# Turning key and value rows on VectorE and through DRAM instead of on TensorE, in a two-layer decoder step

## The chip, the cores and the metric

The kernel runs on one core of one Trainium2 chip. The metric is the device time of one execution in microseconds; a run's figure is the median of several executions. TensorE is the matrix engine (PE in the profile, its weight loads PEld), VectorE is DVE, ScalarE is ACT, GpSimd is POOL, and SyncE is SP, whose queue issues most of the DMAs.

## The reference

A step of a two-layer trunk over 512 prompt tokens and 32 new tokens of eight sequences (544 token columns). Layer 0 mixes tokens by a convolution, layer 1 by an attention without softmax, and each is followed by a gated feed-forward part. The change lies in layer 1, where key and value rows are outputs of their own and values also enter the attention:

```python
qkv = (h @ attn_w_qkv[a]).reshape(b, t, 3, N_HEADS, HEAD_DIM)
q, k, v = qkv[:, :, 0], qkv[:, :, 1], qkv[:, :, 2]
...
z = jnp.einsum('bqhd,bkhd->bhqk', q, k) * (HEAD_DIM ** -0.5)
z = z + bias[None, :, None, None]
log_fail = jnp.where(valid, jax.nn.log_sigmoid(-z), 0.0)
after = lax.cumsum(log_fail, axis=3, reverse=True) - log_fail
weights = jnp.where(valid, jnp.exp(jax.nn.log_sigmoid(z) + after), 0.0)
out = jnp.einsum('bhqk,bkhd->bqhd', weights, v)
...
new_k.append(k)
new_v.append(v)
```

`k_rows_p` and `v_rows_p` are these rows for the prompt: 512 tokens by 1024 features in fp32, one token's features side by side.

## The kernel before

Activations lie with features on the 128 partitions (eight chunks of 128 features) and the 544 tokens along the free dimension. Every projection multiplies fp32 weights as a high and a low part, so a chunk of 128 outputs takes three matmuls for each of eight input chunks. It is done in two halves of tokens, 256 and 288 columns, into PSUM tiles `acc` of which two exist.

The kernel's stages follow each other. Layer 1's attention stage, which holds the whole change, begins with the first key projection (L2126 to L2128) and ends with the output projection's first quarter. In it `Plan` collects operations with an engine, a cost in us, and what they read and write; `run` then walks a clock of its own, takes for each engine the ready operation with the best mix of start and urgency, and emits its instructions at once. So each engine's program order comes out of these costs, and any edit of an operation re-orders all of them. The projections are `fill`: they are taken when nothing else is ready for TensorE. SP's DMAs are operations too (`"sp"`, cost 3.0, the queue free again after 0.7).

For chunk `c` and half `h`, `keys(c, h)` projects, copies the result to `kT` on ScalarE (L2164), and `values(c, h)` copies it to a tile `vT` (L2178). Both then call `to_rows` (L2150): two TensorE transposes of 128x128 (L2156) into the PSUM tile `one`, so that tokens are on partitions. For keys a VectorE copy (L2170) brings the rows to `kr` and one DMA per half (L2171) stores them with runs of 512 bytes. For values a VectorE copy (L2182) brings them to `vtok[c % 3]`, which the attention reads, and one DMA per chunk stores `vtok` (L2185).

`pair(c)` is the prompt's attention for the two heads of chunk `c`: logits (L2388), the weights on ScalarE, GpSimd and VectorE (running sums L2418), transposes of the weights into PSUM tiles `t` (L2430), and `products` (L2450), which multiply them with `vtok`. `page_logits` and `sequence` are the new tokens' attention over cached pages, gathered by GpSimd (L2018) into three buffers; the pages are transposed (L2246) into `t` as well. The PSUM tile `one` also serves the new tokens' small steps. Weights for the projections are loaded by `Ring.load` on SP (L361) into two buffers `raw`, and split into high and low parts (L398 on ScalarE, L401 on VectorE) five slots ahead of their use; the load of a buffer is issued right behind the L401 that reads it last.

Of the kernel before, what the change touches and what calls it, by code (L numbers as in the profile page):

```python
# [9 lines left out]
F32 = mybir.dt.float32  # L10
# [7 lines left out]
P = 128  # L18
D = 1024
NC = D // P  # L20
SEQ = 512
# [13 lines left out]
SA = (0, 256)  # L35
# [215 lines left out]
def tile_trunk(  # L251
# [217 lines left out]
    def uid(s):  # L469
        _n[0] += 1  # L470
        return f"{s}_{_n[0]}"
# [262 lines left out]
    def psum(tag):  # L734
        def make():
            if tag == "acc":
                taken.append(tag)
            return bank(tag, uid(tag))

        return plan.tile(tag, banks[tag], make)  # L740
# [1310 lines left out]
    act_table("natural_log_exp_and_others")  # L2051

    close(ps_cm)
    kpv = k_p[0, 0].rearrange("(b p) h d -> p b (h d)", p=P)
    vpv = v_p[0, 0].rearrange("(b p) h d -> p b (h d)", p=P)
    ksv = k_s.rearrange("o b i h d -> (o b i) (h d)")
    vsv = v_s.rearrange("o b i h d -> (o b i) (h d)")
# [14 lines left out]
    HALF = [slice(0, HD), slice(HD, P)]  # L2072
    ps_cm, ps = open_pool("ps_va", space=PSUM)
    banks.clear()
    banks.update(acc=2, one=1, dz=1, av=1, z=2, t=1)


    plan = Plan()
# [13 lines left out]
    def sbuf(tag, w, bufs, dt=F32, pool_=va):  # L2092
        return plan.tile(tag, bufs, lambda: pool_.tile([P, w], dt, tag=tag, name=uid(tag), bufs=bufs))
# [10 lines left out]
    def acost(n):  # L2104
        return 0.1 + n * 0.95e-3
# [41 lines left out]
            prepare(slot + SPLIT_BUFS)  # L2147
        return pt

    def to_rows(src, r):  # L2150

        rows = psum("one")

        def turn():
            for b in range(2):
                pe.transpose(rows()[:, b * P:(b + 1) * P], src(b), ident)  # L2156

        plan.op("pe", 0.22, turn, r=r, w=[rows])
        return rows, (lambda: rows()[:, :2 * P].rearrange("p (b d) -> p b d", b=2))

    def keys(c, h):
        c0, n = (SA, SB)[h]
        pt = project(k0 + TURNS.index(("k", c)), h)
        plan.op("act", acost(256), lambda: act.copy(kT[:, c, c0:c0 + 256], pt()[:, :256]),  # L2164
                r=[pt], w=[("k", c, h)] + ([("ktp", i) for i in range(4)] if c >= 4 else []))
        if h:
            plan.op("act", 0.2, lambda: act.copy(kT_s[:, c, :], pt()[:, 256:n]), r=[pt], w=[("kT_s", c)])
        rows, src = to_rows(lambda b: kT[:, c, c0 + b * P:c0 + (b + 1) * P], [("k", c, h)])
        kr = sbuf("kr", 2 * P, 2)
        plan.op("dve", 0.38, lambda: dve.tensor_copy(kr().rearrange("p (b d) -> p b d", b=2), src()), r=[rows], w=[kr])  # L2170
        plan.op("sp", 3.0, lambda: nc.sync.dma_start(out=kpv[:, 2 * h:2 * h + 2, c * P:(c + 1) * P],  # L2171
                                                     in_=kr().rearrange("p (b d) -> p b d", b=2)), r=[kr])

    def values(c, h):
        n = (SA, SB)[h][1]
        pt = project(k0 + TURNS.index(("v", c)), h)
        vt = plan.tile("vT", 2, lambda: vts_.tile([P, SA[1]], F32, tag="vT", name=uid("vT"), bufs=2))
        plan.op("act", acost(256), lambda: act.copy(vt(), pt()[:, :256]), r=[pt], w=[vt])  # L2178
        if h:
            plan.op("act", 0.2, lambda: act.copy(vT_s[:, c, :], pt()[:, 256:n]), r=[pt], w=[("vT_s", c)])  # L2180
        rows, src = to_rows(lambda b: vt()[:, b * P:(b + 1) * P], [vt])
        plan.op("dve", 0.38, lambda: dve.tensor_copy(vtok[c % 3][:, 2 * h:2 * h + 2, :], src()),  # L2182
            r=[rows], w=[("vtok", c % 3, h)])
        if h:
            plan.op("sp", 3.0, lambda: nc.sync.dma_start(out=vpv[:, :, c * P:(c + 1) * P], in_=vtok[c % 3]),  # L2185
                    r=[("vtok", c % 3, 0), ("vtok", c % 3, 1)])

    def new_rows(cols, r, dst):

        rows = psum("one")  # L2190

        def turn():
            for g in range(2):
                pe.transpose(rows()[:, g * P:(g + 1) * P], cols(g), ident)

        def store():
            for j in range(4):
                nc.sync.dma_start(out=dst[:, :].rearrange("t (g j d) -> t g j d", g=2, j=4)[:, :, j, :], in_=new_s[32 * j:32 * j + 32])

        plan.op("pe", 0.22, turn, r=r, w=[rows])  # L2200
        plan.op("act", 0.35, lambda: act.copy(new_s, rows()[:, :2 * P].rearrange("p (g d) -> p g d", g=2)),
                r=[rows], w=["new", "Qz"])
        plan.op("sp", 3.0, store, r=["new"])
# [68 lines left out]
                    r=[z], w=[f"Zd{bg}", ("Zd", 2 * bg + g)])  # L2272

    def new_logits():
        zn = psum("one")

        def f():
            for t in range(4):
                bg, g = t // 2, t % 2
                for s in range(4):  # L2280
                    c = 4 * g + s
                    pe.matmul(zn()[32 * s:32 * s + 32, t * NS:(t + 1) * NS], Qf[:, c, bg, :], kT_s[:, c, :],
                              start=(t == 0), stop=(t == 3), skip_group_check=True)

        plan.op("pe", 0.6, f, r=[("kT_s", c) for c in range(NC)], w=[zn], form="c32")
        for t in range(4):
            plan.op("dve", 0.25, lambda t=t: dve.scalar_tensor_tensor(
                Zn[:, t, :], zn()[:, t * NS:(t + 1) * NS], bcol[:, t % 2:t % 2 + 1], mnew[:, t // 2, :],
                op0=ALU.add, op1=ALU.add), r=[zn], w=["Zn"])

    def to_columns(t, pt, src, dst, key, r):

        plan.op("pe", 0.12, lambda: [pe.transpose(pt()[:, i * P:(i + 1) * P], x, ident) for i, x in enumerate(src)], r=r, w=[pt])
        plan.op("act", 0.12 + 0.12 * len(src), lambda: act.copy(dst, pt()[:, :len(src) * P].rearrange("p (g r) -> p g r", r=P)),
                r=[pt, "sd"], w=[(key, t)])

    def decode_weights():
        for i in range(2):
            for eng, cost, f in suffix_steps(Zd[:, 2 * i:2 * i + 2, :], late_sd, KW):
                plan.op(eng, cost, f, w=[f"Zd{i}", "sd", "Qz"])  # L2300
            plan.op("act", 0.6, lambda i=i: act.activation(Zd[:, 2 * i:2 * i + 2, :], Zd[:, 2 * i:2 * i + 2, :], AF.Exp), w=[f"Zd{i}"])
        for t in range(4):
            to_columns(t, psum("one"), [Zd[:, t, pg * P:(pg + 1) * P] for pg in range(2)], wT[:, t], "wT", [f"Zd{t // 2}"])

    def new_weights():
        for eng, cost, f in suffix_steps(Zn, Sn, NS):
            plan.op(eng, cost, f, w=["Zn"])
        plan.op("act", 0.2, lambda: act.activation(nsn, Sn[:, :, 0], AF.Exp, scale=-1.0), r=["Zn"], w=["nsn"])
        for i in range(4):
            rows = slice(32 * i, 32 * i + 32)  # L2310
            plan.op("act", 0.2, lambda rows=rows: act.activation(Zw[rows, :, rows], Zn[rows], AF.Exp), r=["Zn"], w=[("Zw", i)])
        for t in range(0, 4, 2):
            to_columns(t, psum("one"), [Zw[:, t, :], Zw[:, t + 1, :]], wn[:, t:t + 2, :], "wn", [("Zw", i) for i in range(4)])

    def sequence(n):

# [21 lines left out]
    dec = Zd.rearrange("p t k -> p (t k)")[:, 0:512].rearrange("p (c b r) -> p c b r", c=NC, b=NB)  # L2338

    def new_values(bg):  # L2340
        pt, t = psum("dz"), psum("one")
        o = oacc[:, bg, :]

        def new():
            for g in range(2):
                pe.matmul(pt()[:, g * P:(g + 1) * P], wn[:, 2 * bg + g, :], new_s[:, g, :],
                          start=(g == 0), stop=True, skip_group_check=True)

        def turn():
            for g in range(2):  # L2350
                pe.transpose(t()[:, g * P:(g + 1) * P], o[:, g * P:(g + 1) * P], ident)

        plan.op("pe", 0.45, new, r=["new", "pages", ("wn", 2 * bg)], w=[pt])
        for g in range(2):
            cols = slice(g * P, (g + 1) * P)
            plan.op("dve", 0.25, lambda g=g, cols=cols: dve.scalar_tensor_tensor(
                o[:, cols], o[:, cols], nsn[:, 2 * bg + g:2 * bg + g + 1], pt()[:, cols], op0=ALU.mult, op1=ALU.add),
                r=[pt, "nsn"], w=[("oacc", bg)])
        plan.op("pe", 0.25, turn, r=[("oacc", bg)], w=[t])
        plan.op("act", 0.4, lambda: act.copy(  # L2360
            dec[:, :, 4 * bg:4 * bg + 4, :], t()[:, :2 * P].rearrange("p (c b r) -> p c b r", c=NC, b=4)),
            r=[t], w=["Zd0", "Zd1"] + [("Zd", i) for i in range(4)])
# [146 lines left out]
    o0 = slot_no[0]  # L2509
    slot_no[0] += 4  # L2510
    begun = []
    for i, tag in enumerate(("acc", "z", "z", "one")):
        pt = psum(tag)
        begun.append(pt)
        last = None
        for q in range(4):
            last = plan.op("pe", 6 * SA[1] * COL, weighted(pt, o0 + i, 0, q), w=[pt], follows=last,
                           r=[("slot", o0 + i)] + [("X", k) for k in (2 * q, 2 * q + 1)])
# [62 lines left out]
```

## Time and profile before

| | |
|---|---|
| median of 3 executions | 1266.91 us (1265.88 to 1267.45) |
| the profiled execution | 1266.66 us, of which the span 1265.0 us |
| attention stage in the trace | 632 to 845 us |

Busy time and its share of the span are given by engine. A wait is put down to what ended it. The chain of work that ended last is followed back from the last instruction, so an engine with a large share of it sets the time there. Matmuls are pipelined: one starts long before the one ahead of it has ended, so the mean duration of one is no price for an added one; the chain, which counts each instruction only until the next one takes over, is.

### The profile page before, as it was taken

The page shows a single profiled execution, that of the slowest core. Times are in us where ns is not written, and L with a number is a line of the kernel's source. Part 1 is how long each engine was busy: PE and PEld are TensorE (multiplying, and loading weights), DVE is VectorE, ACT ScalarE, POOL GpSimd, SP SyncE. Part 2 cuts the span into 40 slices and gives each one's busy share as a digit, 9 for nine tenths or more (in the row PEclk, how much of TensorE's full clock was granted, in tenths as well). Part 3 has the DMA queues.
Part 4 walks back from the last instruction along what each step waited for, and adds up shares of the span by engine and source line. Part 5 has one row for each costly group of instructions (what it writes and reads, how often), then busy time and mean ns, then how long its engine had stood idle before and what let it go on. Part 6 is the DMA issues. An engine that isn't in the chain of part 4 may idle for free.

```text
span 1265.0 us, 26475 instructions
## 1 busy us (share of the span) xinstructions
PE 1253.8 (99%) x10846; PEld 1203.5 (95%) x10846; DVE 1004.6 (79%) x1696; ACT 717.2 (57%) x1436; POOL 165.6 (13%) x291
## 2 busy tenths in 40 slices
PE   9999999999999999999999999999999999999998
PEld 8997699999999999999989888999999999999997
DVE  7999886988987887869865589766988987887863
ACT  6794584646645455445565498754645645454453
POOL 5000014111001000002042143200111001000000
PEclk9999999999999999999999999999999999999999
DMA  7465423123233233244355544342223233232221
GB/s 215 127 172 151 128 68 116 34 85 118 92 98 114 67 119 105 71 144 171 117 183 152 157 139 137 114 148 71 65 87 110 84 110 117 67 118 88 89 77 72
DMA packets 119179, 142.39 MB, mean 113 GB/s; under 512 B 5101, under 2 KB 110245, under 8 KB 118786
## 3 DMA queue, kind: packets, MB, share of 16 engines
q1 hardware_dynamic: 110350, 111.89, 28.4%
q0 software_dynamic: 8704, 28.80, 7.2%
q8 instruction: 85, 1.39, 0.5%
q14 instruction: 36, 0.29, 0.1%
q10 hardware_dynamic: 4, 0.01, 0.0%
HBM read 129.34 MB, written 12.18 MB: 112 GB/s over the span
## 4 chain that ended last, share of the span: by engine, by line
PE 84%; DVE 13%; ACT 1%; issue 1%; DMA 0%; DVEq 0%; ACTq 0%
PE acc L1632 5%; PE acc L1631 5%; PE acc L1630 5%; PE acc L756 4%; PE acc L757 4%; PE acc L758 4%; PE av L893 3%; PE av L1409 3%; PE av L1410 3%; PE av L1411 3%; DVE wlo L401 3%; PE tr L1410 3%; PE tr L1409 3%; PE tr L1411 3%; PE tr L1630 3%; PE tr L1632 2%
## 5 line engine op out<-in xcount | busy, mean ns | idle before, releaser
L398 ACT CAST whi<-raw 128x1024 fp32r<-128x1024 f32 (+2 forms) x247 | 224.2, 911 | 119.4 <-PE av L1410 24.9
L401 DVE TENSOR_TENSOR wlo<-raw,whi 128x1024 fp32r<-128x1024 f32 (+2 forms) x247 | 259.2, 1052 | 26.1 <-ACT whi L398 24.8
L756 PE MATMUL acc<-XH,whi 128*128 128x288 f32 (+1 forms) x384 | 112.7, 294 | 0.0
L758 PE MATMUL acc<-XH,wlo 128*128 128x288 f32 (+1 forms) x384 | 110.3, 287 | 0.9 <-DVE wlo L401 0.9
L757 PE MATMUL acc<-XL,whi 128*128 128x288 f32 (+1 forms) x384 | 110.3, 287 | 0.0
L1409 PE MATMUL av<-HH,whi 128*128 128x288 f32 (+1 forms) x280 | 83.2, 297 | 0.4 <-DVE xT L1719 0.4
L1410 PE MATMUL av<-HL,whi 128*128 128x288 f32 (+1 forms) x280 | 82.6, 295 | 0.0
L1632 PE MATMUL acc<-TH,wlo 128*128 128x272 f32 x288 | 82.6, 287 | 0.0
L1631 PE MATMUL acc<-TL,whi 128*128 128x272 f32 x288 | 82.6, 287 | 0.0
L1630 PE MATMUL acc<-TH,whi 128*128 128x272 f32 x288 | 82.6, 287 | 0.0
L2126 PE MATMUL acc<-XH,whi 128*128 128x256 f32 (+1 forms) x264 | 82.0, 310 | 0.6 <-ACT kT L2164 0.6
L1411 PE MATMUL av<-HH,wlo 128*128 128x288 f32 (+1 forms) x280 | 82.2, 294 | 0.0
L1666 ACT COPY G<-acc 128x272 f32<-128x272 f32 (+1 forms) x72 | 26.8, 372 | 93.9 <-PE acc L1632 93.9
L1409 PE MATMUL tr<-HH,whi 128*128 128x256 f32 (+1 forms) x280 | 78.6, 281 | 0.0
L1410 PE MATMUL tr<-HL,whi 128*128 128x256 f32 (+1 forms) x280 | 78.4, 280 | 0.0
L1411 PE MATMUL tr<-HH,wlo 128*128 128x256 f32 (+1 forms) x280 | 78.3, 280 | 0.0
L2128 PE MATMUL acc<-XH,wlo 128*128 128x256 f32 (+1 forms) x264 | 75.8, 287 | 0.0
L2127 PE MATMUL acc<-XL,whi 128*128 128x256 f32 (+1 forms) x264 | 75.7, 287 | 0.0
L756 PEld LDWEIGHTS acc<-XH,whi 128*128 128x128 f32 x384 | 72.2, 188 | 1.4 <-issue 0.4
L758 PEld LDWEIGHTS acc<-XH,wlo 128*128 128x128 f32 x384 | 72.1, 188 | 1.1 <-DVE wlo L401 1.1
L757 PEld LDWEIGHTS acc<-XL,whi 128*128 128x128 f32 x384 | 72.2, 188 | 0.3
L1570 DVE SCALAR_TENSOR_TENSOR cv<-G,fprm,cv 128x560 f32<-128x560 f32 x88 | 69.5, 797 | 0.5
(465 smaller groups left out, 4373.8 us busy)
## 6 DMA issues: line engine op xcount, KB each, us to landing
raw<-in_ffn_w_gate_dram SPq DMA_DIRECT2D x22, 1024.0 KB
raw<-in_ffn_w_up_dram SPq DMA_DIRECT2D x22, 1024.0 KB, 5.4
raw<-in_ffn_w_down_dram SPq DMA_DIRECT2D x24, 768.0 KB, 4.6
raw<-in_attn_w_qkv_dram SPq DMA_DIRECT2D x12, 1024.0 KB, 5.3
raw<-in_conv_w_in_dram POOLq DMA_DIRECT2D x6, 1024.0 KB, 6.9
rep<-glu SPq DMA_DIRECT2D x36, 142.0 KB, 2.9
raw<-in_conv_w_out_dram POOLq DMA_DIRECT2D x4, 1024.0 KB, 6.0
raw<-in_ffn_w_down_dram SPq DMA_DIRECT2D x8, 512.0 KB
```

Of the source, the lines that this page charges most:

```text
L398: act.copy(hi[:, k, :], src[:, k])
L401: dve.tensor_tensor(lo[:, k, :], src[:, k], hi[:, k, :], op=ALU.subtract)
L756: pe.matmul(o, hi[:, k, :], XH[:, k, c0:c0 + n], start=(k == 0), stop=False)
L757: pe.matmul(o, hi[:, k, :], XL[:, k, c0:c0 + n], start=False, stop=False)
L758: pe.matmul(o, lo[:, k, :], XH[:, k, c0:c0 + n], start=False, stop=(k == NC - 1))
L1409: pe.matmul(o, hi[:, j + k, :], xh, start=(start and k == 0), stop=False, **kw)
L1410: pe.matmul(o, hi[:, j + k, :], xl, start=False, stop=False, **kw)
L1411: pe.matmul(o, lo[:, j + k, :], xh, start=False, stop=(stop and k == len(xs) - 1), **kw)
L1630: pe.matmul(o, hi[:, j + k, :], xh, start=(start and k == 0), stop=False, **kw)
L1631: pe.matmul(o, hi[:, j + k, :], xl, start=False, stop=False, **kw)
L1632: pe.matmul(o, lo[:, j + k, :], xh, start=False, stop=(k == 3), **kw)
L2126: pe.matmul(o, hi[:, k, :], XH[:, k, c0:c0 + n], start=(k == 0), stop=False)
```

## The change

Keys: one VectorE transpose (of 32x32 blocks within the tile) per half from `kT` to `kr`, which now is one tile of 512 columns with a single buffer; after the second half four DMAs (one for each 32 features) store a chunk in runs of 128 bytes. Values: one VectorE transpose per half, straight from PSUM, into `vT`, also 512 columns and a single buffer; four DMAs write it to a DRAM scratch tile `vrows` in runs of 128 bytes, a fifth loads `vtok` from there, and a sixth stores `vtok` as before. The TensorE transposes, the copies to `vT` and the tile `one` are gone, and `t` has two PSUM tiles instead of one.

```diff
-    banks.update(acc=2, one=1, dz=1, av=1, z=2, t=1)
+    banks.update(acc=2, dz=1, av=1, z=2, t=2)
...
-    def to_rows(src, r):
-        rows = psum("one")
-        def turn():
-            for b in range(2):
-                pe.transpose(rows()[:, b * P:(b + 1) * P], src(b), ident)
-        plan.op("pe", 0.22, turn, r=r, w=[rows])
-        return rows, (lambda: rows()[:, :2 * P].rearrange("p (b d) -> p b d", b=2))
+    krs, vbs = {}, {}

     def keys(c, h):
...
-        rows, src = to_rows(lambda b: kT[:, c, c0 + b * P:c0 + (b + 1) * P], [("k", c, h)])
-        kr = sbuf("kr", 2 * P, 2)
-        plan.op("dve", 0.38, lambda: dve.tensor_copy(kr().rearrange("p (b d) -> p b d", b=2), src()), r=[rows], w=[kr])
-        plan.op("sp", 3.0, lambda: nc.sync.dma_start(out=kpv[:, 2 * h:2 * h + 2, c * P:(c + 1) * P],
-                                                     in_=kr().rearrange("p (b d) -> p b d", b=2)), r=[kr])
+        if not h:
+            krs[c] = sbuf("kr", SEQ, 1)
+        kr = krs[c]
+        plan.op("dve", 0.08 + 256 * 1.06e-3, lambda: dve.transpose(kr()[:, c0:c0 + 256], kT[:, c, c0:c0 + 256]), r=[("k", c, h)], a=[kr])
+
+        def store():
+            for a in range(4):
+                rows = slice(32 * a, 32 * a + 32)
+                nc.sync.dma_start(out=k_p[0, 0].rearrange("(b i) h d -> i b (h d)", i=32)[:, :, c * P + 32 * a:c * P + 32 * a + 32],
+                                  in_=kr()[rows].rearrange("i (b j) -> i b j", j=32))
+
+        if h:
+            plan.op("sp", 3.0, store, r=[kr])

     def values(c, h):
...
-        plan.op("act", acost(256), lambda: act.copy(vt(), pt()[:, :256]), r=[pt], w=[vt])
...
-        rows, src = to_rows(lambda b: vt()[:, b * P:(b + 1) * P], [vt])
-        plan.op("dve", 0.38, lambda: dve.tensor_copy(vtok[c % 3][:, 2 * h:2 * h + 2, :], src()),
-            r=[rows], w=[("vtok", c % 3, h)])
...
+        if not h:
+            vbs[c] = plan.tile("vT", 1, lambda: vts_.tile([P, SEQ], F32, tag="vT", name=uid("vT"), bufs=1))
+        vb = vbs[c]
+        plan.op("dve", 0.1 + 256 * 1.06e-3, lambda: dve.transpose(vb()[:, c0:c0 + 256], pt()[:, :256]), r=[pt], a=[vb])
...
+        d = plan.tile("vrows", 2, lambda: scratch.tile([SEQ, P], F32, tag="vrows", name=uid("vrows"), bufs=2))
+
+        def away():
+            for a in range(4):
+                rows = slice(32 * a, 32 * a + 32)
+                nc.sync.dma_start(out=d()[:, rows].rearrange("(b i) j -> i b j", i=32),
+                                  in_=vb()[rows].rearrange("i (b j) -> i b j", j=32))
+
+        plan.op("sp", 3.0, away, r=[vb], w=[d])
+        plan.op("sp", 3.0, lambda: nc.sync.dma_start(out=vtok[c % 3], in_=d().rearrange("(b p) d -> p b d", p=P)),
+                r=[d], w=[("vtok", c % 3, 0), ("vtok", c % 3, 1)])
...
-        rows = psum("one")
+        rows = psum("t")
```

The new tokens' other steps (`new_logits`, `to_columns`, `new_values` and one group of the output projection) take `t` in place of `one` in the same way.

SP's queue before, around the chunk 3 of the values, whose store is the first row with `vtok_8070` (the names are buffers: `kr` key rows, `raw` a weight buffer; the brackets hold what the row waits for, `DVE` being VectorE and `DMAHW` an earlier DMA):

```order
L361 DMA raw_9237<-in_attn_w_o_dram 128x8x256 [waits DMAHW4_49,DMAHW1_49,DVE_49]
L2171 DMA out_dram<-kr_9422 128x2x128 [waits DVE_49]
L2171 DMA out_dram<-kr_9456 128x2x128 [waits DMAHW3_49,DVE_49]
L2185 DMA out_dram<-vtok_8070 128x4x128 [waits DVE_49]
L2171 DMA out_dram<-kr_9618 128x2x128 [waits DMAHW5_49,DVE_49]
L361 DMA raw_9631<-in_attn_w_o_dram 128x8x256 [waits DMAHW6_49,DMAHW0_49,DVE_49]
```

The same place of SP's queue after the change, again for chunk 3 of the values:

```order
L2187 DMA vrows_9460<-vT_9361 32x16x32 [waits DMAHW4_49,DVE_49]
L2187 DMA vrows_9460<-vT_9361 32x16x32 [waits DMAHW5_49]
L2187 DMA vrows_9460<-vT_9361 32x16x32 [waits DMAHW6_49]
L2187 DMA vrows_9460<-vT_9361 32x16x32 [waits DMAHW7_49]
L361 DMA raw_9486<-in_attn_w_o_dram 128x8x256 [waits DMAHW0_49,DVE_49]
L2191 DMA vtok_8070<-vrows_9460 128x4x128 [waits DMAHW5_49,DMAHW6_49,DMAHW4_49,DMAHW7_49,DMAHW1_49,PE_49]
L2166 DMA out_dram<-kr_9546 32x16x32 [waits DMAHW2_49,DVE_49]
L2166 DMA out_dram<-kr_9546 32x16x32 [waits DMAHW3_49]
L2193 DMA out_dram<-vtok_8070 128x4x128 [waits DMAHW1_49]
```

Nothing but stores and weight loads stood in the queue; now the load of `vtok`, which TensorE reads, stands behind four small writes and a weight load of 1 MB. Chunk 4 has the same rows in the same order (`vrows_9723`, `raw_9771`, `vtok_8071`).

VectorE after the change, from the transpose of chunk 3's second half on (`s` is a running sum, `e` the weights, `wlo` the low part of a weight slot):

```order
L2178 STREAM_TRANSPOSE vT_9361<-acc_9397 128x256
L2426 SCALAR_TENSOR_TENSOR s_9437<-ones,s_9437 128x384 x2
L401 TENSOR_TENSOR wlo_9458<-raw_8832,whi_9457 128x1024
L2426 SCALAR_TENSOR_TENSOR s_9437<-ones,s_9437 128x128 x2
L2431 TENSOR_TENSOR e_9404<-e_9404,s_9437 128x1024
L2161 STREAM_TRANSPOSE kr_9546<-kT 128x256 x2
```

The weight load `raw_9486` above waits for the third of these rows, which reads its buffer last; it stands two running sums behind the transpose for which the four writes wait.

TensorE before, a place with two of the removed pairs of transposes (L2156) among the other work:

```order
L2430 MATMUL t_9407<-ident,e_9189 128x128 x4
L2156 MATMUL one_9412<-ident,kT 128x128 x2
L2388 MATMUL z_9415<-kT,qT 128x384
L2388 MATMUL z_9417<-kT,qT 128x384
L2388 MATMUL z_9415<-kT,qT 128x128
L2388 MATMUL z_9417<-kT,qT 128x128
L2430 MATMUL t_9429<-ident,e_9275 128x128 x4
L2156 MATMUL one_9436<-ident,kT 128x128 x2
```

TensorE after, down to the first product of chunk 3 (`av_9566`, which reads `vtok_8070`):

```order
L2438 MATMUL t_9548<-ident,e_9404 128x128 x4
L2438 MATMUL t_9553<-ident,e_9404 128x128 x4
L2125 MATMUL acc_9522<-XH,whi_8823 128x288
L2126 MATMUL acc_9522<-XL,whi_8823 128x288
L2127 MATMUL acc_9522<-XH,wlo_8824 128x288
L2125 MATMUL acc_9522<-XH,whi_8823 128x288
L2126 MATMUL acc_9522<-XL,whi_8823 128x288
L2127 MATMUL acc_9522<-XH,wlo_8824 128x288
L2458 MATMUL av_9566<-e_9176,vtok_8070 64x128 x8
```

No pair of row transposes is left, the weights are transposed two tiles at a time, and the products of chunk 3 follow the second half of its value projection (`acc_9397`) by 48 projection matmuls, four groups of weight transposes and one `sequence` (32 matmuls in the trace).

More of the change, by code (lines that the diff above doesn't have):

```diff
@@ L2053, in tile_trunk @@
     close(ps_cm)
-    kpv = k_p[0, 0].rearrange("(b p) h d -> p b (h d)", p=P)
     vpv = v_p[0, 0].rearrange("(b p) h d -> p b (h d)", p=P)
@@ L2174, in values @@
     def values(c, h):
-        n = (SA, SB)[h][1]
+        c0, n = (SA, SB)[h]
         pt = project(k0 + TURNS.index(("v", c)), h)
[L2177 to L2180, printed above, removed]
-        rows, src = to_rows(lambda b: vt()[:, b * P:(b + 1) * P], [vt])
@@ L2182, in values @@
-        plan.op("dve", 0.38, lambda: dve.tensor_copy(vtok[c % 3][:, 2 * h:2 * h + 2, :], src()),
-            r=[rows], w=[("vtok", c % 3, h)])
-        if h:
-            plan.op("sp", 3.0, lambda: nc.sync.dma_start(out=vpv[:, :, c * P:(c + 1) * P], in_=vtok[c % 3]),
-                    r=[("vtok", c % 3, 0), ("vtok", c % 3, 1)])
+        if not h:
+            vbs[c] = plan.tile("vT", 1, lambda: vts_.tile([P, SEQ], F32, tag="vT", name=uid("vT"), bufs=1))
+        vb = vbs[c]
+        plan.op("dve", 0.1 + 256 * 1.06e-3, lambda: dve.transpose(vb()[:, c0:c0 + 256], pt()[:, :256]), r=[pt], a=[vb])
@@ new lines, in values @@
+        if not h:
+            return
+        plan.op("act", 0.2, lambda: act.copy(vT_s[:, c, :], pt()[:, 256:n]), r=[pt], w=[("vT_s", c)])
+        d = plan.tile("vrows", 2, lambda: scratch.tile([SEQ, P], F32, tag="vrows", name=uid("vrows"), bufs=2))
[4 more added lines that the diff above has]
+                                  in_=vb()[rows].rearrange("i (b j) -> i b j", j=32))
@@ L2188, in new_rows @@
+        plan.op("sp", 3.0, away, r=[vb], w=[d])
+        plan.op("sp", 3.0, lambda: nc.sync.dma_start(out=vtok[c % 3], in_=d().rearrange("(b p) d -> p b d", p=P)),
+                r=[d], w=[("vtok", c % 3, 0), ("vtok", c % 3, 1)])
+        plan.op("sp", 3.0, lambda: nc.sync.dma_start(out=vpv[:, :, c * P:(c + 1) * P], in_=vtok[c % 3]),
+                r=[("vtok", c % 3, 0), ("vtok", c % 3, 1)])
     def new_rows(cols, r, dst):
-        rows = psum("one")
+        rows = psum("t")
         def turn():
@@ L2274, in new_logits @@
     def new_logits():
-        zn = psum("one")
+        zn = psum("t")
         def f():
@@ L2302, in decode_weights @@
         for t in range(4):
-            to_columns(t, psum("one"), [Zd[:, t, pg * P:(pg + 1) * P] for pg in range(2)], wT[:, t], "wT", [f"Zd{t // 2}"])
+            to_columns(t, psum("t"), [Zd[:, t, pg * P:(pg + 1) * P] for pg in range(2)], wT[:, t], "wT", [f"Zd{t // 2}"])
     def new_weights():
@@ L2312, in new_weights @@
         for t in range(0, 4, 2):
-            to_columns(t, psum("one"), [Zw[:, t, :], Zw[:, t + 1, :]], wn[:, t:t + 2, :], "wn", [("Zw", i) for i in range(4)])
+            to_columns(t, psum("t"), [Zw[:, t, :], Zw[:, t + 1, :]], wn[:, t:t + 2, :], "wn", [("Zw", i) for i in range(4)])
     def sequence(n):
@@ L2340, in new_values @@
     def new_values(bg):
-        pt, t = psum("dz"), psum("one")
+        pt, t = psum("dz"), psum("t")
         o = oacc[:, bg, :]
@@ L2511, in tile_trunk @@
     begun = []
-    for i, tag in enumerate(("acc", "z", "z", "one")):
+    for i, tag in enumerate(("acc", "z", "z", "t")):
         pt = psum(tag)
```

## Prediction

> **What bounds the kernel now.** I read the page from the top, then the attention stage alone (632 to 845 us), since every changed line runs there.
>
> ```profile
> span 1265.0 us, 26475 instructions
> PE 1253.8 (99%) x10846; PEld 1203.5 (95%) x10846; DVE 1004.6 (79%) x1696; ACT 717.2 (57%) x1436; POOL 165.6 (13%) x291
> PEclk9999999999999999999999999999999999999999
> ```
>
> TensorE is busy all the time at full clock. The next rows are from the view by windows (width, then busy us and instructions of PE, PEld, DVE, ACT, POOL, then clock, DMA share and GB/s), and the last is the chain of waits of that stage by line.
>
> ```profile
> 632.00:845.00 213.00, 211.95 (x2121) 188.85 (x2120) 149.73 (x222) 144.10 (x257) 60.03 (x71) 1.00 0.47 149
> ...
> 720.00:740.00 20.00, 20.00 (x187) 17.69 (x188) 18.24 (x25) 16.39 (x29) 6.30 (x7) 1.00 0.36 117
> 740.00:760.00 20.00, 20.00 (x238) 16.36 (x238) 17.92 (x26) 17.98 (x29) 7.57 (x8) 1.00 0.54 170
> 760.00:780.00 20.00, 19.63 (x223) 16.98 (x220) 18.92 (x27) 17.08 (x31) 11.28 (x11) 1.00 0.53 165
> ...
> by line: PE acc L2126 14.3%; PE acc L2127 13.5%; PE acc L2128 13.5%; PE z L2388 9.5%; PE av L2450 8.8%; PE t L2430 8.4%; PE t L2246 6.7%; PE dz L2326 3.8%; PE dz L2264 3.3%; PE one L2156 3.1%; DVE s L2418 2.1%; DVE e L2423 1.1%; PE z L2126
> ```
>
> In the stage PE is busy 211.95 of 213 us: work left out of it shortens the kernel, and a wait put into its queue lengthens it, one for one. VectorE has room on average (149.7 of 213) but little from 720 to 780 (55.1 of 60). The removed transposes, L2156, hold 3.1% of the stage's chain, 6.6 us.
>
> **What is removed from TensorE.** In the stage's groups the pairs of transposes and the copies around them are (line, engine, names, count, then busy us and mean ns of one):
>
> ```profile
> L2170 DVE COPY kr<-one 128x256 f32<-128x256 f32 x16 | 6.7, 418 | 13.8 <-PE one L2156 13.8
> L2182 DVE COPY vtok<-one 128x256 f32<-128x256 f32 x16 | 6.7, 416 | 4.5 <-PE one L2156 4.5
> ...
> L2156 PE MATMUL one<-ident,vT 128*128 128x128 f32 x32 | 6.3, 280 | 0.5 <-DVE kr L2170 0.4
> L2156 PE MATMUL one<-ident,kT 128*128 128x128 f32 x32 | 6.1, 272 | 0.0
> L2178 ACT COPY vT<-acc 128x256 f32<-128x256 f32 x16 | 6.0, 376 | 7.2 <-PE acc L2128 7.0
> ```
>
> The 64 transposes' 12.4 us of busy time overlap their neighbours. What one pair costs in line is read from the chain from 767 to 781 us (start, us, what):
>
> ```profile
> 773.20 0.59 PE t L2430 x4
> 773.78 0.22 PE one L2156 x2
> 774.00 1.01 PE dz L2326 x32
> 775.01 1.07 PE z L2388 x8
> ...
> 778.30 0.44 PE t L2430 x4
> ```
>
> 32 pairs at 0.22 are **7.0 us saved**. That ScalarE loses the 16 copies to `vT` (6.0 us) I cost at nothing: it does not bound the stage.
>
> **VectorE.** 32 copies become 32 transposes of the same 128x256. No row shows such an instruction. From below it takes 0.17 us (a quarter of the 0.69 of L2407 on 1024 columns, quoted below), from above twice the copy, 0.84; I take the copy's 0.42, the same shape, hence no change. At 0.84 the cover goes first from 720 to 780 us, where 9 of the copies lie and VectorE has 4.9 us of idle time: 9 x 0.42 = 3.8 us. [...]
>
> **The values' new way.** `vtok` now comes over transpose, four writes, a load queued behind a weight load, and only then the products. I count from t0, the end of the transpose. Rows of SP's timeline and of the landing times (issue to landing, min/median/max) of `kr` stores, weight loads and page gathers, in this order:
>
> ```profile
> 764.57 0.38 SPq L361 DMA_DIRECT2D raw<-in_attn_w_o_dram  x1
> 769.34 0.37 SPq L2171 DMA_DIRECT2D out_dram<-kr  x1
> ...
> 806.38 2.64 SPq L2198 DMA_DIRECT2D out_dram<-xT  x4
> ...
> DMA to landing us min/median/max: 1.8/1.9/3.9
> ...
> DMA to landing us min/median/max: 4.5/5.8/10.3
> ...
> DMA to landing us min/median/max: 4.2/5.4/8.9
> ```
>
> Four issues take 1.5 (4 x 0.37) to 2.6 us (the row of 806); I take 1.8, with the last landing 1.9 after its issue at 1.4 to 2.0, so at t0 + 3.6. The load of 256 KB has twice the packets of a `kr` store; I take 2.4 for its 1.9. Without company `vtok` is there at t0 + 6.2 with the semaphores between. How small packets are priced comes from the queue rows, first of the stretch 674.9 to 677.2 us with one `kr` store in it, then of the page (packets, MB, share of 16 engines):
>
> ```profile
> q1 hardware_dynamic: 272, 0.13, 20.3%
> ...
> q1 hardware_dynamic: 110350, 111.89, 28.4%
> ```
>
> That is 0.203 x 16 x 2.3 / 272 = 27.5 ns for 478 bytes, and 0.284 x 16 x 1265 / 110350 = 52 ns for 1014. On that line 128 bytes cost 11 ns; the other end is no gain at all below 512, 27.5 ns. 2048 packets of a chunk then take 1.4 or 3.5 us of the 16 engines; I take 1.4, which the four landings already cover. The 32,768 packets of the stage make 23 us (56 at the other end) beside a DMA share of 0.47 x 213 = 100.
>
> [...]
>
> **Where TensorE waits for it.** The orders show the products of chunks 3 and 4 close behind their values. The prices, from the timeline of VectorE and the windows:
>
> ```profile
> 721.57 1.22 DVE L401 TENSOR_TENSOR wlo<-raw,whi 128x1024 fp32r<-128x1024 f32 x1
> 724.03 1.94 DVE L2418 TENSOR_TENSOR_SCAN s<-ones,s 128x384 f32<-128x384 f32 x2
> 747.63 2.33 DVE L2418 TENSOR_TENSOR_SCAN s<-ones,s 128x512 f32<-128x512 f32 x2
> 751.71 0.69 DVE L2407 TENSOR_SCALAR e<-e 128x1024 f32<-128x1024 f32 x1 [0.30 <-POOL e L2402]
> 752.32 1.22 DVE L2423 TENSOR_TENSOR e<-e,s 128x1024 f32<-128x1024 f32 x1
> ...
> 722.30:726.30 4.00, 4.00 (x33) 4.00 (x32) 3.96 (x6) 2.65 (x6) 0.55 (x1) 1.00 0.57 177
> ```
>
> Projection matmuls are 4.00 / 33 = 0.12 us apart. Chunk 3: between the end of its value projection and its products TensorE has 48 of them (5.8), four groups of weight transposes (4 x 0.44) and one `sequence` (1.01), **8.6 us**. The transpose ends 1.8 us after the projection (0.2 of semaphores, 0.42 itself, and I take one instruction of 1.2 ahead of it; 0.7 to 2.4 is possible). The weight load is issued after two running sums and the low part (1.94 + 1.22 = 3.2), ahead of the load of `vtok` at 3.6; by its median it lands at t0 + 9.0, and the 512 packets behind it need 0.9 more: t0 + 9.9. That a small DMA sits out a weight load is seen above: the store of 769.34, issued behind the load of 764.57, is the one with 3.9 us to landing. So `vtok` is there 1.8 + 9.9 = 11.7 us after the projection, **3.1 us too late** (0.7 with every bound at its low end, 4.5 us of load; 8 at 10.3).
>
> Chunk 4 has the same queue, but its weight load waits for a product, two sums of 512 and the low part: 1.22 + 2.33 + 1.22 = 4.8. Then 4.8 + 5.8 + 0.9 = 11.5, with 1.8 in front 13.3, against 48 matmuls, two groups, a `sequence` and logits of 1.07, 8.8 us: 4.5, less 1.0 since VectorE catches up in the first wait, **3.5 us** (2 to 9). Behind both products TensorE's queue holds the next chunk's logits and projections; its order is fixed, nothing fills in, so the waits count in full.
>
> Chunks 0 and 7 have no weight load in between: by the same prices t0 + 6.2 meets 8.9 us of room at chunk 0; at chunk 7 (7.7 us) the new tokens' four stores, 2.64 us, go first and leave about 0.5 late. Chunks 1, 2, 5 and 6 have 16 us or more. With two `t` tiles the page transposes come closer: a third page is asked for again only 5.6 us after its buffer was freed, twice by the same prices, against a gather's 5.4 to landing; I take 0.8. Together 1.3.
>
> `kr` with one buffer: chunk 4's first transpose waits for chunk 3's last store, which SP issues late; VectorE waits 1 us or so there (0 to 2). The second `t` tile should take away about as much of VectorE's waits for `t`. I set both at nothing.
>
> **Sum.** 1266.7 (the profiled execution, 0.02% under the median of 1266.9) - 7.0 + 3.1 + 3.5 + 1.3 = **1267.6 us**, no change. A difference under 0.2%, 2.5 us, is about what a measurement of this kernel can't tell from none: 1264.4 to 1269.4.
>
> **Rivals.**
> - *The round trip hides*: the weight loads come through in 4.5 us and VectorE takes the transposes at once; chunks 3 and 4 wait 0.7 and 2 or less. For it: the stage's DMA share is 0.47. Against: gathers run in the same stretch. 1266.7 - 7.0 + 0 to 4 = 1260 to 1264, faster.
> - *Short runs cost the DMA engines as much as runs of 512 or twice that*: slower, decided by the packet price, from about 27 ns on. 2048 packets take 3.5 us instead of 1.4, which each of the four tight chunks (0, 3, 4, 7) waits for: 4 x 2.1 on 1267.6 is 1276; at 55 ns 4 x 5.6, 1290. Against: the price falls along the two rows quoted.
> - *VectorE becomes the bound* in its dense stretch: transposes at 0.84 us give 1267.6 + 3.8 = 1271.4.
> - *Weight loads at their slow end*, 8 us under gathers: 2.2 more on each of two chunks, 1272.
>
> That the transposes leave TensorE is certain from the order; that the stage then ends earlier is what is open.
>
> **How the numbers follow.** Forecast 0.38 (its own range 1264.4 to 1269.4, no change). Hidden round trip 0.27, all of it faster. Short runs 0.14, VectorE 0.11, slow loads 0.10, all slower. So faster 0.27, same 0.38, slower 0.35. The range leaves out half of the dearest short runs and the last tenth of the fast end: 1261 to 1276.
>
> **What would show it.** TensorE at L2458 waiting for the DMA `vtok` twice, at chunks 3 and 4, for 3 us each, and almost nowhere else; STREAM_TRANSPOSE near 0.42 us; the four writes landed 3.6 us after the transpose; `vtok` landing about 1 us behind the weight load. If those waits are missing, the time is near 1260; if packets of 128 bytes take 27 ns or more, waits at chunks 0 and 7 join in. The forecast is wrong if TensorE waits at other places than L2458, for pages or for VectorE, for more than 2 us in all.

## The result, and the profile after

The changed kernel takes 1282.24 us (median of 5, 1279.67 to 1283.73) beside 1266.36 us for the kernel before (1265.67 to 1267.45): ratio 1.0125, 95% interval 1.0114 to 1.0135. It is slower by 1.25%, 16 us; the forecast was 1267.6, no change.

The page of the profiled execution (1283.73 us): span, busy time by engine, granted clock in 40 slices, and the main DMA queue (packets, MB, share of 16 engines).

```profile
span 1281.4 us, 26412 instructions
PE 1254.0 (98%) x10782; PEld 1202.0 (94%) x10782; DVE 1003.6 (78%) x1696; ACT 712.8 (56%) x1420; POOL 162.8 (13%) x291
PEclk9999999999999999999999998999999999999999
q1 hardware_dynamic: 144014, 116.09, 30.2%
```

TensorE has 64 matmuls less (10782 for 10846), yet as much busy time as before. One slice of the clock's row is below 9, and the queue carries 33,664 packets more for 4.2 MB more.

The view by windows, of the attention stage and of the stretches shown of before; then TensorE's waits in that stage (in total, times, longest).

```profile
632.00:860.00 228.00, 211.86 (x2062) 187.10 (x2062) 150.29 (x225) 141.45 (x244) 57.55 (x72) 0.98 0.56 157
720.00:740.00 20.00, 16.11 (x160) 13.58 (x159) 14.87 (x21) 13.68 (x25) 5.98 (x8) 0.91 0.55 151
740.00:760.00 20.00, 19.67 (x218) 17.30 (x219) 14.92 (x22) 14.00 (x21) 9.30 (x9) 1.00 0.74 215
760.00:780.00 20.00, 17.50 (x203) 14.88 (x202) 10.02 (x14) 11.22 (x20) 5.40 (x7) 1.00 0.63 172
780.00:800.00 20.00, 16.01 (x149) 14.08 (x149) 11.47 (x17) 8.77 (x14) 2.15 (x3) 0.83 0.42 121
...
PE av L2458 <- DMA vtok<-vrows: 6.5, 2, 4.0
PE t L2438 <- DVE e L2431: 3.9, 1, 3.9
PE t L2438 <- ACT e L2441: 1.8, 2, 1.5
PE acc L495 <- DVE xT L2542: 1.8, 1, 1.8
PE t L2254 <- DMA xT<-in_cache_k_dram,idx: 0.6, 1, 0.6
```

The waits sum to 16.0 us with one of 0.5 and three of 0.3 that are not shown; the same view of before has two, 0.6 and 0.4. So 15.0 us of waits are new. The 1.5 us at L2438 (third row, ending at 846.9 us) wait for a copy of ScalarE near the stage's end; no edit below was aimed at them. VectorE, dense before from 720 to 780 (55.1 of 60), is now idle for a third of it (39.8): it waits too.

The transposes themselves cost what was forecast (groups of the stage: count, busy us, mean ns, idle time before them):

```profile
L2178 DVE STREAM_TRANSPOSE vT<-acc 128x256 f32<-128x256 f32 x16 | 7.2, 447 | 9.3 <-ACT vT_s L2181 7.1 <-PE acc L2127 1.7 <-DMA out_dram<-kr 0.5
L2161 DVE STREAM_TRANSPOSE kr<-kT 128x256 f32<-128x256 f32 x16 | 7.0, 438 | 17.8 <-DMA out_dram<-kr 8.7 <-ACT kT L2154 7.4 <-ACT e L2261 1.7
```

The second row's releaser is new: VectorE sat 8.7 us waiting for stores of key rows, 3.83 us of it at chunk 1 (until 648.7 us), behind which TensorE waits 0.3 us twice, and 4.87 us at chunk 4. TensorE's 3.9 us at L2438 come from the latter. VectorE's timeline (start, us, what, idle time ahead of it) and then SP's:

```profile
727.66 0.68 DVE L2415 TENSOR_SCALAR e<-e 128x1024 f32<-128x1024 f32 x1
733.21 0.45 DVE L2161 STREAM_TRANSPOSE kr<-kT 128x256 f32<-128x256 f32 x1 [4.87 <-DMA out_dram<-kr]
733.58 1.18 DVE L2431 TENSOR_TENSOR e<-e,s 128x1024 f32<-128x1024 f32 x1
...
723.95 0.38 SPq L2191 DMA_DIRECT2D vtok<-vrows  x1
724.38 1.04 SPq L2166 DMA_DIRECT2D out_dram<-kr  x2
727.00 0.39 SPq L2193 DMA_DIRECT2D out_dram<-vtok  x1
727.43 12.50 SPq L2166 DMA_DIRECT2D out_dram<-kr  x5
```

Chunk 4's first transpose may not write `kr` until chunk 3's fourth store has read it. SP holds that store behind the store of `vtok`, which waits for `vtok` to land, and issues it at 727.43; VectorE is released 5.7 us later. The weights of L2431, which TensorE needs, stand behind the transpose in VectorE's queue.

Why so late? The DMA queues from 727.4 to 733.1 us, page gathers first, SP's queue second:

```profile
q0 software_dynamic: 283, 1.03, 57.6%
q1 hardware_dynamic: 1056, 0.33, 23.3%
```

Gathers and SP's queue together keep the 16 engines busy four fifths of the time there: the store shares them.

The last loss is not a wait but a clock. Windows of 4 us at three places (the clock is the third number from the end):

```profile
736.00:740.00 4.00, 4.00 (x47) 3.30 (x45) 4.00 (x5) 2.02 (x3) 0.00 (x0) 0.57 0.22 35
...
788.00:792.00 4.00, 2.63 (x26) 2.63 (x28) 1.42 (x2) 0.00 (x0) 0.00 (x0) 0.50 0.64 131
792.00:796.00 4.00, 4.00 (x54) 2.83 (x52) 0.00 (x0) 1.35 (x3) 0.00 (x0) 0.71 0.03 5
856.00:860.00 4.00, 2.24 (x15) 2.04 (x14) 2.14 (x6) 1.58 (x4) 0.00 (x0) 0.90 0.00 0
860.00:864.00 4.00, 4.00 (x23) 4.00 (x22) 0.69 (x2) 0.82 (x1) 0.00 (x0) 0.67 0.00 0
```

Of the waits there (731.02 to 734.91, 785.38 to 789.37, 856.53 to 858.29 us) the clock falls 1.4 us behind the end of the first, 1.9 us ahead of the end of the second and 0.9 us behind the end of the third. An estimate of the loss from these rows is busy time times the missing clock: 1.7 + 1.3 + 1.2 + 0.2 + 1.3 = 5.7 us.

### The profile page after: what moved, and what is told of

It reads as the page before. It is cut to its first block, busy times and chain, and to the rows that moved or that the text cites. A ratio compares the mean times of both kernels' runs of the same rounds, so it can differ in the third digit from the quotient of the medians.

```text
span 1281.4 us, 26412 instructions
## 1 busy us (share of the span) xinstructions
PE 1254.0 (98%) x10782; PEld 1202.0 (94%) x10782; DVE 1003.6 (78%) x1696; ACT 712.8 (56%) x1420; POOL 162.8 (13%) x291
## 4 chain that ended last, share of the span: by engine, by line
PE 78%; DVE 14%; DMA 3%; issue 2%; ACT 2%; POOL 0%; SPq 0%; DVEq 0%; ACTq 0%; POOLq 0%
PE acc L1632 5%; PE acc L1631 5%; PE acc L1630 5%; PE acc L756 4%; PE acc L757 4%; PE acc L758 3%; PE av L893 3%; PE av L1409 3%; PE av L1410 3%; PE av L1411 3%; PE tr L1410 3%; DVE wlo L401 3%; PE tr L1409 3%; PE tr L1411 3%; PE tr L1630 2%; PE tr L1632 2%
## 5 line engine op out<-in xcount | busy, mean ns | idle before, releaser
L1630 PE MATMUL acc<-TH,whi 128*128 128x272 f32 x288 | 82.6, 287 | 0.0
```

Source lines behind the costliest of these rows:

```text
L1630: pe.matmul(o, hi[:, j + k, :], xh, start=(start and k == 0), stop=False, **kw)
```

## The experiments

The theory (A in the expectations): the loss is three separate causes of waiting (the stores of `kr`, the loads of `vtok`, the bank at L495) with the half clock behind them, and the 32 pairs left out are a real gain underneath. The rivals are crowded queues (B), lateness that a repaired wait only hands on (C, D), and a new order that trades one wait for another (E). All ratios are to the kernel before on the same chip (1266.3 to 1266.5 us).

| run | median us | ratio, 95% interval |
|---|---|---|
| kr2: two buffers for key rows | 1273.02 | 1.0051 (1.0038 to 1.0065) |
| begun: the quarter's last tile in a bank of acc | 1278.23 | 1.0102 (1.0086 to 1.0117) |
| vfirst: weight loads behind the load of `vtok` | 1275.28 | 1.0070 (1.0057 to 1.0084) |
| long: runs of 512 bytes | 1274.87 | 1.0064 (1.0051 to 1.0078) |
| fix3: kr2, begun and vfirst together | 1264.32 | 0.9985 (0.9976 to 0.9994) |
| fix3c: the same, the plan told the price | 1263.39 | 0.9977 (0.9968 to 0.9986) |
| keys2: before, only keys changed | 1265.36 | 0.9992 (0.9983 to 1.0001) |
| values: before, only values changed | 1270.99 | 1.0039 (1.0025 to 1.0053) |
| banks: before, only PSUM tiles changed | 1269.35 | 1.0023 (1.0013 to 1.0032) |

### kr2

```diff
-            krs[c] = sbuf("kr", SEQ, 1)
+            krs[c] = plan.tile("kr", 1, lambda: va.tile([P, SEQ], F32, tag="kr", name=uid("kr"), bufs=2))
```

> The changed kernel (1282.2 us) with two buffers for the key rows instead of one; every engine's order stays as it is. Theory A (waits at named places): VectorE's wait of 4.87 us at 728 us for the stores of kr goes, and with it TensorE's idle 3.78 us at 731 us and the 3.41 us at half clock right behind it (1.7 us lost): 5.5 us less, 1276.7, if the later waits stay. Rival B (the DMA queues are crowded by runs of 128 bytes, and the wait only shows it at one buffer): the stores land as late as before, and what was saved is waited for at vtok of chunk 3: within 1.5 us of 1282.2.

1273.0, 9.2 us less. VectorE waits for no store of `kr` any more. TensorE's two largest waits in the stage:

```profile
PE av L2458 <- DMA vtok<-vrows: 7.3, 2, 4.6
PE acc L495 <- DVE xT L2542: 1.8, 1, 1.8
```

Every engine's order is that of the changed kernel. The 3.9 us at L2438 are gone, as A says; 0.8 of it comes back at L2458. The gain is larger than 5.5. The five times run from 1271.4 to 1276.8, and the profiled execution is the slowest of them; its span is 6.5 us shorter, and it has two stretches of 3.41 us at half clock instead of the 13.65 us of the changed kernel. One of the stretches that went stood behind the wait for `kr`, as A counts it; the other is half of the 6.83 us behind the second wait for `vtok`, which A did not forecast and this edit does not explain. Rival B's form of it, the wait handed on whole, is out.

### begun

```diff
-        pt = psum(tag)
+        pt = psum(tag) if i < 3 else plan.tile("t", 2, lambda: ps.tile([P, 512], F32, tag="acc", name=uid("acc"), bufs=2))
```

> The changed kernel (1282.2 us) with the fourth tile of the output projection's first quarter in a bank of acc instead of one of t, so that the tile that L495 opens does not reuse its bank. Theory A: TensorE's idle 1.76 us at 856 us goes, and the 3.41 us at half clock from 859 us on with it (1.7): 3.5 us less, 1278.7. Rival C (the stage's last weights are late, and L495 waits for them by whatever tile): the wait moves to another row, the time stays within 1 us of 1282.2.

1278.2, 4.0 us less, where A said 3.5; the four times spread from 1275.0 to 1281.3, so that the row that goes says more than the size. The wait at L495 is not in the view of waits any more, and nothing replaces it (the largest of this run):

```profile
PE av L2458 <- DMA vtok<-vrows: 5.1, 2, 2.7
PE t L2438 <- DVE e L2431: 3.7, 1, 3.7
```

The mechanism is a shared bank: L495 opens the first tile `acc` of the pool that follows, and in the changed kernel it starts when VectorE has read the quarter's last tile, `t`, which it adds to `xT` last of four (the two rows of the changed kernel):

```profile
857.82 0.42 DVE L2542 TENSOR_TENSOR xT<-t,xT 128x256 f32<-128x256 f32 x1
858.29 0.40 PE L495 MATMUL acc<-XH,whi 128*128 128x288 f32 x1 [1.76 <-DVE xT L2542]
```

Before, the last of the quarter was `one`, and L495 started at 844.03 us, ahead of VectorE's read of `one` at 845.82. In this run it starts at 851.52 us, ahead of that read at 852.98.

### vfirst

```diff
+    def behind(f):
+        with tc.issue_after(held[1]) if held[1] else ExitStack():
+            f()
...
-                    self.load()
+                    (late_.append if held[0] else lambda f: f())(lambda: behind(self.load))
...
+    def fetch_(c, d):
+        held[1] = nc.sync.dma_start(out=vtok[c % 3], in_=d().rearrange("(b p) d -> p b d", p=P)).ins
+        held[0] -= 1
+        while late_ and not held[0]:
+            late_.pop(0)()
```

`held[0]` counts the chunks whose second value transpose is queued and whose load of `vtok` is not. Lines from here on are up to 16 higher: L2458 is L2473, L361 L366, L2438 L2453.

> The changed kernel (1282.2 us) in which no weight load is issued on SP between a chunk's four writes of vrows and its load of vtok: the weight load goes behind it. Only SP's order changes. Theory A: the load of vtok no longer sits behind 1 MB; it lands 2.5 to 3 us after its issue, as at 723.95 us, instead of 6.4 and 6.7, so the waits of L2458 (2.5 and 3.99 us) and the half clock behind the second (2.5 us lost) go: about 9 us less, 1273, with up to 2 us of other waits in place of them. Rival B (short runs and page gathers make the landing late, not the weight load): it still lands 5 us or more after its issue, and under 3 us are gained, 1279 or more.

1275.3, 7.0 us less. First the path to the products of chunk 3 in the changed kernel (the chain of waits: start, us), then SP's timeline of this run, then its waits.

```profile
755.02 2.81 DMA vrows<-vT
...
757.90 6.40 DMA vtok<-vrows
...
758.10 0.38 SPq L2157 DMA_DIRECT2D vtok<-vrows  x1
758.56 0.46 SPq L366 DMA_DIRECT2D raw<-in_attn_w_o_dram  x1
762.30 0.38 SPq L2208 DMA_DIRECT2D out_dram<-vtok  x1
...
780.67 0.38 SPq L2157 DMA_DIRECT2D vtok<-vrows  x1
781.14 0.46 SPq L366 DMA_DIRECT2D raw<-in_attn_w_o_dram  x1
783.80 0.38 SPq L2208 DMA_DIRECT2D out_dram<-vtok  x1
...
PE t L2453 <- DVE e L2446: 3.9, 1, 3.9
...
PE av L2473 <- DMA vtok<-vrows: 0.9, 2, 0.5
```

The store of `vtok` leaves when its load has landed, so the load took 4.2 and 3.1 us here, against 6.4 and 6.7 behind a weight load (5.4 to 7.3 in kr2, begun and long, where the weight load still stands ahead). TensorE's wait fell from 6.5 to 0.9, and the half clock behind the second wait (6.83 us) is gone. A's mechanism holds, though the loads land later than its 2.5 to 3 us. L2269 (page transposes) waits 1.2 and 1.0 us here, at 650 and 683 us; that is ahead of the first place where SP's order differs (700 us), so the edit did not make these waits.

### long

```diff
-in_=kr()[rows].rearrange("i (b j) -> i b j", j=32))
+in_=kr()[rows].rearrange("i (b j) -> i b j", j=P))
...
-in_=vb()[rows].rearrange("i (b j) -> i b j", j=32))
+in_=vb()[rows].rearrange("i (b j) -> i b j", j=P))
```

The output sides of these DMAs take 4 whole rows of 128 features in the same way.

> The changed kernel (1282.2 us) with the same DMAs, bytes and orders of TensorE, VectorE, ScalarE and GpSimd, but each write of vrows and each store of kr in runs of 512 bytes instead of 128; the rows land at wrong places, so the turning by 32x32 blocks is left incomplete. Theory A (12 to 15 ns a short packet): the four writes land about 1 us sooner, each of the two waits at L2458 and the one for kr is 1 us shorter: 1279 to 1280. Rival B (short runs cost the DMA engines a multiple of their bytes): the waits at L2458 and for kr mostly go, 1272 or less.

1274.9, 7.4 us less, between the two. Its two largest waits:

```profile
PE av L2458 <- DMA vtok<-vrows: 4.9, 2, 2.6
PE acc L495 <- DVE xT L2542: 1.8, 1, 1.8
```

The waits of VectorE's key transposes for stores of `kr` are gone, with one buffer. But the edit moved more than the run length, and this run does not price that alone:

- SP's order differs. The load of `vtok` of chunk 2 now stands ahead of the key stores (718.40 us, instead of 723.95 behind the first of them), so chunk 3's last key store leaves 2.8 us after the start of the transpose that it waits for, instead of 4.5. It landed 1.8 us after its issue, against 5.7, with the gathers at 15% of the engines' time around it instead of 58%.
- ScalarE has two neighbours the other way round near the stage's end, other than the expectation says, and the 1.5 us that TensorE waits there in the changed kernel are missing here.
- The second wait for `vtok` is 1.6 us shorter (2.38 us). In begun, where no DMA was touched, it is 2.37, so this is no sign of the run length.

Where the orders are still equal and gathers run in both, at chunk 1, the run length does tell: VectorE waited 3.83 us there for a store that landed 4.5 us after its issue, and here it waits for ScalarE alone. So short runs made the stores of `kr` later there; how much of the 4.87 us at chunk 4 is theirs stays open, and between A and B nothing is decided.

How dear is a short packet alone? The four writes of chunk 0, with nothing beside them, from 670.2 to 673.8 us in the changed kernel, then from 669.1 to 672.3 us in this run:

```profile
q1 hardware_dynamic: 2112, 0.26, 48.7%
...
q1 hardware_dynamic: 576, 0.26, 42.1%
```

0.487 x 16 x 3.6 / 2112 = 13.3 ns each, where the prediction had 11 and, as the other end, 27.5; and 0.421 x 16 x 3.2 / 576 = 37.4 ns for 512 bytes (64 smaller packets are in both counts). In all 28 us of the engines' time against 22: short runs cost 1.3 times as much for the same bytes.

### The parts of the change by themselves: keys2, values, banks

`keys2` and `values` take over `keys` or `values` of the changed kernel as the change's diff has it, keys with kr2's line; `banks` is the change's `banks.update` line and its six other places with `t` for `one`, and `to_rows` on `t` as well.

> The kernel before (1266.5 us) with only the keys turned by VectorE, kr in two buffers of 512 columns, stores in runs of 128 bytes; the values, the PSUM tiles one and t as before. Theory A: 16 pairs of TensorE transposes less, 16 x 0.22 = 3.5 us, and nothing that TensorE waits for hangs on the keys' stores: 1263. Rival B (33 thousand short packets, here half of them, crowd the queues that weights and pages come by): 1266 or more, with waits for xT or raw.

> The kernel before (1266.5 us) with only the values turned by VectorE and fetched back through DRAM; keys, PSUM tiles one and t as before. Theory A: 16 pairs less (3.5 us), against it the waits for vtok at chunks 3 and 4 (6.5 us) and a half clock behind the longer one (1.7 to 2.5): 1266.5 - 3.5 + 8.5 = 1271.5, within 2. Rival C (only the single kr buffer and the shared PSUM bank cost): 1264 or less.

> The kernel before (1266.5 us) with only the PSUM tiles changed: no one, two t in its place, whose users take t. Theory A: the output projection's first L495 meets a bank of t that VectorE still reads, 1.76 us and 1.71 at half clock, as in the changed kernel: 1270. Rival C (two t tiles loosen the weights' and pages' transposes by as much): 1265 to 1267.

The waits of TensorE, in this order, and last the row of values' wait for `vtok`:

```profile
PE acc L2126 <- ACT kT L2166: 1.9, 1, 1.9
PE acc L495 <- DVE xT L2544: 0.9, 1, 0.9
...
PE av L2462 <- DMA vtok<-vrows: 3.4, 1, 3.4
PE acc L2126 <- ACT kT L2164: 1.9, 1, 1.9
...
PE acc L495 <- DVE xT L2534: 1.8, 1, 1.8
PE t L2351 <- DVE oacc L2356: 1.1, 1, 1.1
...
836.41 0.91 PE L2462 MATMUL av<-e,vtok 128*64 128x128 f32 x6 [3.37 <-DMA vtok<-vrows]
```

Values alone lose 4.6 us, where A said 5.0, but not by A's terms. The plan is ordered anew, and at chunks 3 and 4 TensorE does not wait. The only wait for `vtok` is 3.4 us at the last chunk, 7, whose load stands behind the four writes and the new tokens' four stores (issued at 833.54 us); 1.9 us at the key projection come besides, each with 3.41 us at half clock. That the number agrees is luck. The run shows that the values' way costs more than its 16 pairs of transposes save, and rival C is out. The tiles alone lose 3.0, which are the tiles' two rows; A's 3.5 had the first of them and a half clock that did not come. Keys alone gain 1.0 where A said 3.5, with an interval that reaches no change: the re-ordered plan has 1.9 us at the first row's place, where before had 0.6, and 3.41 us at half clock behind it. Nothing of B's (waits for `xT` or `raw`) shows, and neither theory had its size.

### fix3 and fix3c

fix3 has the three edits above. fix3c changes two costs of the plan besides:

```diff
-        plan.op("sp", 3.0, away, r=[vb], w=[d])
-        plan.op("sp", 3.0, lambda: fetch_(c, d),
+        plan.op("sp", 4.5, away, r=[vb], w=[d])
+        plan.op("sp", 3.5, lambda: fetch_(c, d),
```

> The changed kernel with the three edits of the runs kr2, begun and vfirst together: two buffers kr, the weight loads of SP behind the loads of vtok, the last tile of the first quarter out of t's banks. Theory A (the loss is those three waits with their half clock, and they add): 1282.2 - 9.2 - 4.0 - 7.0 = 1262.0, and the 7.0 us that TensorE no longer does then show as some 4 us under the kernel before (1266.5). Rival D (the waits stand in one another's shadow, or the single buffer and the weight loads are paid for later): 1267 or more.

> The kernel of the run fix3 (1264.3 us) with the plan told what the values' way takes: cost 4.5 us instead of 3.0 for the four writes, 3.5 instead of 3.0 for the load of vtok. The plan then puts the tight products a little later. Theory A: the 1.8 us in which L2473 still waits for vtok go, 1262.5 to 1263. Rival E (any new order trades one short wait for another): within 1.5 us of 1264.3, with other waits in its place.

fix3 is 17.9 us under the changed kernel; the three single gains sum to 20.2. They nearly add, and the sign turns: 0.15% under the kernel before. D's 1267 is out. fix3c is 0.23% under the kernel before, the fastest here. Its page, and its waits in the stage:

```profile
span 1262.0 us, 26415 instructions
...
PE t L2453 <- ACT e L2456: 1.5, 1, 1.5
PE dz L2349 <- DMA xT<-in_cache_v_dram,idx: 1.0, 1, 1.0
```

No wait for `vtok` is left among the rows of this view, as A says. Of the 1.8 us, 0.8 comes back at the two rows shown (1.0 and 0.7 in fix3); in all the waits fall from 5.2 to 3.6 us. The time, 0.9 us less, misses A's 1262.5 to 1263 and is within E's 1.5, and the intervals of fix3 and fix3c overlap: which of the two is faster stays open. The 1.5 us at L2453 are those of the changed kernel's third row of waits. Neither execution has a stretch at half clock in the stage.

## Why the prediction was wrong, step by step

- **Removed from TensorE, 7.0 us.** The mechanism is right, the size a little high. fix3c's span is 3.0 us under that of before with 2.6 us more of waits (3.6 against 1.0) and no half clock, so the pairs were worth about 5.6; fix3 gives 6.1 by the same sum (1.9 under, 4.2 more of waits). That is 0.18 to 0.19 us a pair from one execution each, instead of the chain's 0.22; where the rest went was not traced.
- **VectorE at the copy's 0.42 us.** Right: 0.438 and 0.447.
- **Short packets at 11 ns.** 13.3 alone, near enough. The price here is small: 1.3 times the engines' time of 512-byte runs for the same bytes (28 us against 22, long). Beside gathers it was not measured alone.
- **Waits for `vtok` at chunks 3 and 4, 3.1 and 3.5 us.** Measured 2.5 and 3.99, by the mechanism named, a weight load of 1 MB ahead (vfirst). Chunk 3's `vtok` landed 10.8 us after its transpose (753.50 to 764.30), forecast 9.9. These terms stood, with some luck in the sizes: both loads of `vtok` landed about 1 us later after their transposes than forecast (10.8 and 12.6 for 9.9 and 11.5), and the products were due 1.5 and 0.6 us later as well. The 0.2 us for semaphores ahead of the transpose no run shows (0.02 us in the chain of the changed kernel, at 776.29 us); from the landed writes to the issue of the load it was 0.07 and 0.19. One premise was misread. The store of `kr` with 3.9 us to landing is not that of 769.34, for which the trace has no landing, but that of 701.03: it was issued 8.4 us behind its weight load, with page gathers on 61% of the engines' time (701 to 705 us). What moved beside it were gathers, not a weight load; that a weight load ahead delays the load of `vtok`, vfirst showed (4.2 and 3.1 us to landing without one, 6.4 and 6.7 with it).
- **Chunks 0 and 7 and the pages, 1.3 us.** L2458 waits at no other chunk by more than 0.25 us; L2254 for pages 0.6. About right.
- **`kr` with one buffer, "at nothing".** This is the step that failed first. The place was named (chunk 4's first transpose, for chunk 3's last store), its price was put at 1 us, at most 2, and set off against the second `t`. It was 4.87 us on VectorE and 3.9 on TensorE, 1.7 more at half clock. The only landing that the prediction works with for such stores is 1.9 us, the median of 512-byte runs; with 128-byte runs beside page gathers it was 5.7, and the misread store of 701.03 had already taken 3.9 beside gathers. And what stood behind the transpose on VectorE, the weights that TensorE needs next, was not priced at all.
- **The bank of L495.** Not in the forecast: 1.76 us (begun, banks), and 1.5 more at half clock in the changed kernel. The prediction asked what the second `t` does within the stage and not who takes the bank after it.
- **ScalarE's copy at L2438.** Not in the forecast: 1.5 us. It stays in fix3c, and no run takes it apart.
- **The clock.** Not in the forecast: 5.7 us. Every wait was counted at its own length.

The sum by what was measured: 15.0 of waits + 5.7 of clock - 5.8 = 14.9, against 16.4 between the two spans. Of the other 1.5 us, 0.5 lie ahead of the stage, where nothing was changed (a matmul of L1630 with the same 0.49 us of wait starts at 629.24 us before and at 629.70 after). The first L495 starts 14.3 us later than before, so 2.1 of the 16.4 us lie behind it, 1.5 of them clock. That leaves 0.6 behind the stage and 0.4 within it that were not traced. Waits too short for the view are not the place: in the stage's 228 us TensorE is idle for 16.1, and the view has 16.0.

Of the rivals, none is what happened. L2458 did wait; VectorE did not become the bound; short packets at 13.3 ns stayed far from 27 ns, the rival's 55 no run shows, and L2458 does not wait at chunks 0 and 7. Slow weight loads come nearest: from the issue of the weight load to the landed `vtok` it was 8.0 and 7.7 us, where the forecast had 6.7, but the two waits together (6.5) are no longer than forecast (6.6). The last sentence of the prediction had the condition: it is wrong if TensorE waits elsewhere than at L2458 for more than 2 us. It was 9.5.

## What to carry to other kernels

A tile whose buffers go from two to one is a wait of its reader's whole DMA, priced by when that DMA is issued and how it lands in its own run length beside the traffic of that moment, and it holds everything that is queued behind on the waiting engine: here 5.7 us from the last store's issue to its landing, 4.87 us of wait on VectorE and 3.9 on TensorE. A load that the bound engine needs should not stand in a queue behind a bulk load that nobody needs yet; moving only SP's order was worth 7 us here. When PSUM tiles are merged, look also at which banks the next pool takes first (1.76 us here).

## What the runs showed of the hardware that was not expected

Some waits of TensorE cost more than their length: in the changed kernel the granted clock is 0.50 for 3.41 us behind the wait of 3.89 us, for 6.83 us from within the wait of 3.99 us on, and for 3.41 us behind that of 1.76 us, by the estimate above 5.7 us in all. The waits of 1.7 us and more in the profiled execution of each kernel (the stretches are from the trace's clock records; in the changed kernel, windows of 1 us inside them, from 737, 788 and 860 us on, show a clock of 0.50):

| wait us | kernel | half clock, us |
|---|---|---|
| 3.89, 2.50, 3.99, 1.76 | changed | 3.41, 0, 6.83, 3.41 |
| 2.72, 4.55, 1.76 | kr2 | 0, 3.41, 3.41 |
| 3.71, 2.74, 2.37 | begun | 6.83, 0, 0 |
| 3.90, 1.76 | vfirst | 3.41, 3.41 |
| 2.55, 2.38, 1.76 | long | 3.41, 0, 3.41 |
| 1.94, 3.37 | values | 3.41, 3.41 |
| 1.93 | keys2 | 3.41 |
| 1.76 | banks | 0 |

All six waits over 3 us had it, of the 13 of 1.7 to 2.8 us seven. Every stretch in the table is 3.41 us long or twice that. A wait of 1.76 us has one in the changed kernel, in kr2, vfirst and long, and none in banks; what decides below 3 us stays open. The half clock may also be why the changed kernels with waits left spread wider (kr2 over 5.4 us) than those without (fix3c over 2.0); that was not tested.
